# A two-layer trunk on one core: the first up projection's channels in two parts, and one more column group in the first quarter

## The chip, the cores and the metric

The kernel runs on one core of a Trainium2 chip, as one launch. The metric is the time of an execution in microseconds on the device; the smaller the better.

## The reference

The trunk has two layers on 256 tokens of 2048 channels, all in float32. The first layer mixes tokens by pooling, the second by attention; each ends with a gated feed-forward part with a convolution of width 3. A conditioning vector gives each layer six vectors of 2048 numbers, in this order: shift, scale and gate of the mixer (chunks 0, 1, 2), shift, scale and gate of the feed-forward part (chunks 3, 4, 5).

```python
cond = silu(c)
for i in range(2):
    mod = cond @ w_ada[i] + b_ada[i]              # 2048 x 12288
    sh1, sc1, g1, sh2, sc2, g2 = split(mod, 6)
    h = rmsnorm(x, norm_g[i, 0]) * (1 + sc1) + sh1
    y = pool_mixer(h) if i == 0 else moba_attention(h)
    x = x + g1 * y
    h = rmsnorm(x, norm_g[i, 1]) * (1 + sc2) + sh2
    u = causal_conv3(h @ w_up[i]) + conv_b[i]     # 2048 x 11264
    val, gate = split(u, 2)
    x = x + g2 * ((silu(gate) * val) @ w_down[i]) # 5632 x 2048
return rmsnorm(x, final_g)
```

The pool mixer handles four groups of 512 channels with one matrix each.

## The kernel before

Tokens stand transposed: channels on the partitions, 256 tokens along the row (`xT`). All weights, some 554 MB, are read once, in loads of 1 MB on SyncE's queue, into five tiles that take turns (`raw`, `RAW` = 5): load number n+5 waits until load n's tile has been read by its last reader. The program is a list of events, each a load and its use. `later` and `at` hang further work on an event. A scheduler then sets the order of instructions on each engine, each engine works in that fixed order, and semaphores hold it where data or a tile is missing.

**The conditioning stage** comes first. A chunk of the conditioning is made in slices of 512 channels: four loads (`slice_load`, tile `ws<chunk>_<slice>_<quarter>`) of four blocks of 128 rows each. A block is multiplied by its column of `cond` and added up either on VectorE (`accs`, 128x512) or, for the blocks in `PE_BLOCKS`, on TensorE (`row`, one matmul of one row of 512). `mods` matmuls turn the sums into columns and `mod_done` adds the bias. The slices run 3, 2, 1, 0 and each takes the chunks 1, 0, 2. With chunks 1 and 0 of a slice the pool group can be made (`pool_h`, `pool_sums`, `pool_less`, and 32 instructions `pp` of `pool_product` on TensorE), with chunk 2 its output is added to `xT` (`pool_out`), and `squares` collects the squares for the next norm. Then `x1` makes the norm's factor (`ms`, `st_*`, `rrow`). Slice 0 of chunks 4 and 3 follows in eight loads, and then the first step of the dense stream.

**The dense stream.** A step takes one megabyte of weights, 512 rows by 512 columns: ACT rounds it in two halves (`hi`), VectorE makes the rest (`lo`), and TensorE issues 48 matmuls on `h` (`uv` for value columns, `ug` for gate columns). `hi` and `lo` have four buffers each (`HB`), and products run two halves behind (`LAG`). The first up projection of layer 0 goes through `FIRST` = 11 column groups four times, once per quarter of its 2048 rows (K), since the conditioning of the later channels isn't there yet. The sums of the first `HOMES` = 10 groups leave PSUM after each quarter (`to_home`: ACT copies the first quarter, VectorE adds the others to `home`), the eleventh stays in PSUM. Slices 1 to 3 of chunks 3 and 4 come as pairs between these steps, eight loads a slice, all on VectorE (`accs` 128x1024). `h_blocks` makes four blocks of `h` for each quarter (`ht` on VectorE, `h` on ACT, the low part on VectorE). In the last quarter the steps alternate with those of two more groups (`MIX`), and the convolutions of finished groups run beside. After that all products are step by step, layer after layer.

Most instructions are recorded at line 50 of the profile (the helper that issues them), so rows are told apart by their tiles.

Of the kernel before, what the change touches and what calls it, by code (L numbers as in the profile page):

```python
# [17 lines left out]
P = 128  # L18
# [38 lines left out]
def trunk(ctx: ExitStack, tc: tile.TileContext, x, c, norm_g, w_ada, b_ada, pool_w, pool_scale, w_qkv, w_o,  # L57
          rel_table, w_up, conv_w, conv_b, w_down, final_g, out):
    nc = tc.nc
# [19 lines left out]
    PE_BLOCKS = ((2, 5, 8, 11, 14), (3, 7, 11, 15), (2, 4, 6, 9, 11, 13, 15), (2, 5, 7, 10, 13, 15), ())  # L79
    RAW, HB, LAG, T4, PRIO = 5, 4, 2, 6, 1000  # L80

# [160 lines left out]
    def slice_load(ch, s, q, pair):  # L242
# [10 lines left out]
        return load  # L253

    def slice_use(ch, s, q, pair):

        on_pe = PE_BLOCKS[ch if ch < 3 else 3 if s == 0 else 4]
        nk, w = (2, 2) if pair else (4, 1)

        def use(r):  # L260
            if q == 0:
                ada["n"] = ada.get("n", -1) + 1
                if ada["n"] == 0:
                    ada["acc"] = wt([P, D], "acc", 1, "accs")
                if on_pe:
                    ada["row"] = [bank(f"row{ch}_{s}_{j}") for j in range(w)]
            odd = ada["n"] % 2
# [14 lines left out]
            if nk * (q + 1) == KD:  # L282
                with tc.high_priority(offset=2 * PRIO):
                    if on_pe:
                        for j in range(w):
                            ac.activation(row[0:1, j * C:(j + 1) * C], ps[j][0:1, :], AF.Copy)
                    ps = ada["ps", ch, s] = aux(f"mods{ch}_{s}")
# [150 lines left out]
    def group_T(src, nk, c0, rhs, done, name, home=None, each=None):  # L438
# [27 lines left out]

        def products(f, k, hi, lo):
            o = part(f)
            first = k % 4 if home else k
            for kk in range(2):  # L470
# [4 lines left out]
                pe.matmul(o, lo[:, kk, w], h[:, 0:S], start=False,  # L475
                                 stop=(k + kk == nk - 1 or (home is not None and first + kk == 3)),
                                 skip_group_check=True)

        def use_of(k0):
# [73 lines left out]
    PARTS = ((0, 4), (4, 8), (8, NG))  # L553
    HOMES, FIRST, LEAD = 10, 11, 3
    REST, MIX, PRE, SPARE = 1, 2, 2, 2
    QUIET, LATE, START = 7, -0.2, 61

    def ffn(l):
        led = 0
        for pi, (ga, gb) in enumerate(PARTS):  # L560
# [46 lines left out]
            if pi == 0:  # L607
# [3 lines left out]
                if l == 0 and MIX:  # L611
# [402 lines left out]

    later = {}
    for s in range(4)[::-1]:
        e0 = len(events)
        for n, e in enumerate(e for ch in (1, 0, 2) for e in slice_events(ch, s, False)):
            event(*e)
            if n == 5:  # L1020
                event(pool_load(s), lambda r: None)
        e1 = len(events)
        at(e0 + 5, lambda s=s: slice_done(1, s, False))
        at(e0 + 9, lambda s=s: slice_done(0, s, False))
        at(e0 + 9, lambda s=s: pool_h(s))
        at(e0 + 10, lambda s=s: pool_sums(s))
        at(e0 + 10, lambda s=s: pool_less(s))
        for f in range(GB):
            at(e0 + 10 + f, lambda s=s, f=f: pool_product(s, f))
        at(e1 + 1, lambda s=s: slice_done(2, s, False))  # L1030
        at(e1 + 1, lambda s=s: pool_out(s))
        at(e1 + 2, lambda s=s: squares(s * GB, GB, s == 3))
        at(e0 + 1, {3: pool_start, 2: lambda: load_conv(0), 1: lambda: load_conv(1), 0: bias_rows}[s])

# [5 lines left out]

    at(e1 + 3, x1)
    slices = [slice_events(4, 0, False) + slice_events(3, 0, False)] + [slice_events(3, s, True) for s in range(1, 4)]
    for e in slices[0]:
        event(*e)
    at(len(events) - 3, lambda: slice_done(4, 0, False))
    i = 0
    for s in range(4):
        nxt = slices[s + 1] if s < 3 else []
        for g in range(FIRST):
            event(w_load(i), w_use(i))  # L1050
            i += 1
            if g == 0:
                at(len(events) - 1, lambda s=s: (slice_done(3, s, s > 0), h_blocks(0, 1, 4 * s, 4)))
            while nxt and (FIRST - SPARE) * (8 - len(nxt)) < 8 * (g + 1):
                event(*nxt.pop(0))
# [34 lines left out]
    FAST, MANY = 40, 14  # L1090
    PE_ON, VE_ON, AC_ON = (), (59, 60, 61), (55, 59, 60, 61)
    first_main = 200
# [40 lines left out]
```

## Time and profile before

| | us |
|---|---|
| median of 3 runs | 2071.87 (2071.46 to 2075.88) |
| the profiled execution | 2076.08 |
| its span in the profile | 2074.3 |
| TensorE busy | 2013.0 |
| VectorE busy | 1641.4 |
| ACT busy | 960.2 |

The profile shows one execution. Its span runs from the first to the last instruction; 1.78 us of that execution's time lie around it. The mean granted clock of TensorE over the span is 0.981.

### The profile page before, as it was taken

The numbers are of one execution on the slowest core, as the hardware profiler recorded it, in microseconds if no ns is written. First come the engines' busy times: TensorE is split into PE (matmuls) and PEld (weight loads), VectorE is DVE, ScalarE is ACT, GpSimd is POOL, SyncE is SP. The second block draws the span as 40 slices with busy tenths as digits, with TensorE's granted clock in tenths as the row PEclk, the third lists the DMA queues.
The fourth block names the chain that finished last, engine by engine and source line by source line (L and its number), as shares of the span: only waits on it lengthen the run. The fifth ranks groups of instructions, "written<-read, shape, count | busy, mean of one in ns | idle before, by whom it ended". The sixth has DMA issues, their size and how long they took to land. (4 is left out here: it accounts for less than half of the span.)

```text
span 2074.3 us, 38497 instructions
## 1 busy us (share of the span) xinstructions
PE 2013.0 (97%) x16292; PEld 1907.9 (92%) x16292; DVE 1641.4 (79%) x2023; ACT 960.2 (46%) x1206; POOL 12.0 (1%) x64
## 2 busy tenths in 40 slices
PE   6898999999999999999999999999999999999998
PEld 2445999999999999999989889999999999999998
DVE  6887899899889999997787887879885666556666
ACT  3112534566454345444444444446543555435454
POOL 1000000000000000000000000000000000000000
PEclk8988999999999999999999999999999999999999
DMA  9998999655997989896888788678875555556551
GB/s 355 346 363 324 345 346 326 222 191 196 336 360 279 377 320 320 305 324 213 311 288 326 265 308 313 223 250 284 280 268 187 200 195 192 197 189 200 187 202 62
DMA packets 236445, 558.78 MB, mean 269 GB/s; under 512 B 9272, under 2 KB 9592, under 8 KB 221680
## 3 DMA queue, kind: packets, MB, share of 16 engines
q1 hardware_dynamic: 234800, 553.17, 75.4%
q8 instruction: 127, 2.08, 0.4%
q0 software_dynamic: 896, 2.49, 0.3%
q10 hardware_dynamic: 576, 0.67, 0.1%
q14 instruction: 46, 0.38, 0.0%
HBM read 554.17 MB, written 2.12 MB: 268 GB/s over the span
## 5 line engine op out<-in xcount | busy, mean ns | idle before, releaser
L50 DVE TENSOR_TENSOR lo<-w,hi 128x1024 fp32r<-128x1024 f32 x656 | 790.9, 1221 | 260.0 <-ACT hi L50 259.1
L50 ACT ACTIVATE hi<-w 128x1024 fp32r<-128x1024 f32 x656 | 683.2, 1059 | 630.5 <-PE d L50 185.6
L50 PE MATMUL uv<-h,hi 128*128 128x256 f32 x2816 | 485.1, 278 | 3.8 <-ACT h L50 3.8
L50 PE MATMUL d<-act,hi 128*128 128x256 f32 x2816 | 482.0, 277 | 0.6 <-ACT hi L50 0.6
L50 PE MATMUL ug<-h,hi 128*128 128x256 f32 x2816 | 481.8, 276 | 0.0
L50 PEld LDWEIGHTS uv<-h,hi 128*128 128x128 f32 x2816 | 426.6, 189 | 4.5 <-ACT h L50 4.1
L50 PEld LDWEIGHTS d<-act,hi 128*128 128x128 f32 x2816 | 424.9, 188 | 0.9 <-ACT hi L50 0.8
L50 PEld LDWEIGHTS ug<-h,hi 128*128 128x128 f32 x2816 | 424.0, 188 | 0.0
L50 PE MATMUL d<-act,lo 128*128 128x256 f32 x1408 | 387.4, 277 | 4.0 <-DVE lo L50 4.0
L50 PE MATMUL uv<-h,lo 128*128 128x256 f32 x1408 | 387.9, 277 | 0.0
L50 PE MATMUL ug<-h,lo 128*128 128x256 f32 x1408 | 386.3, 276 | 0.0
L50 PEld LDWEIGHTS d<-act,lo 128*128 128x128 f32 x1408 | 263.9, 188 | 4.8 <-DVE lo L50 4.8
L50 PEld LDWEIGHTS uv<-h,lo 128*128 128x128 f32 x1408 | 265.1, 189 | 0.0
L50 PEld LDWEIGHTS ug<-h,lo 128*128 128x128 f32 x1408 | 263.5, 188 | 0.0
L50 DVE SCALAR_TENSOR_TENSOR acc<-wa,cond,acc 128x2048 f32<-128x2048 f32 x105 | 246.3, 2346 | 6.6 <-DMA wa<-in_w_ada_dram 6.3
L50 DVE SCALAR_TENSOR_TENSOR accs<-ws,cond,accs 128x512 f32<-128x512 f32 (+1 forms) x179 | 157.4, 882 | 17.2 <-ACT accs L50 7.9
L50 PE MATMUL k<-h,hi 128*128 128x256 f32 x512 | 93.7, 285 | 1.1 <-ACT h L50 1.1
L50 PE MATMUL row<-ws,cond 128*1 128x512 f32 x152 | 81.5, 663 | 8.3 <-DMA ws<-in_w_ada_dram 8.3
L50 PE MATMUL q<-h,hi 128*128 128x256 f32 x512 | 88.7, 278 | 0.0
L50 PE MATMUL wo<-o,hi 128*128 128x256 f32 x512 | 88.3, 277 | 0.0
L50 PEld LDWEIGHTS k<-h,hi 128*128 128x128 f32 x512 | 80.1, 191 | 2.3 <-ACT h L50 1.4
L50 PE MATMUL v<-hi,h 128*128 128x512 f32 x256 | 80.1, 394 | 0.0
(157 smaller groups left out, 1753.9 us busy)
## 6 DMA issues: line engine op xcount, KB each, us to landing
w<-in_w_up_dram SPq DMA_DIRECT2D x176, 1024.0 KB, 5.1
wa<-in_w_ada_dram SPq DMA_DIRECT2D x112, 1024.0 KB, 5.8
w<-in_w_down_dram SPq DMA_DIRECT2D x88, 1024.0 KB, 5.1
ws<-in_w_ada_dram SPq DMA_DIRECT2D x56, 1024.0 KB, 7.6
w<-in_w_qkv_dram SPq DMA_DIRECT2D x48, 1024.0 KB, 6.4
ws<-in_w_ada_dram SPq DMA_DIRECT2D x48, 512.0 KB, 6.5
w<-in_w_o_dram SPq DMA_DIRECT2D x16, 1024.0 KB, 6.8
pw<-in_pool_w_dram SPq DMA_DIRECT2D x4, 1024.0 KB, 9.0
```

Source lines behind the costliest of these rows:

```text
L50: ins = call(*args, **kwargs)
```

## The change

The last two slices of chunks 0 to 2 are taken in another order: chunks 1 and 0 of slice 1, chunks 1 and 0 of slice 0, then chunk 2 of slice 1 and of slice 0. The squares of slice 0 are no longer added on VectorE but summed by eight more `ms` matmuls.

Slice 0 of chunks 4 and 3 comes in two parts of 256 channels (`half_load`, tiles `wh<slice>_<part>_<quarter>`), each with four loads of 1 MB in two transfers with runs of 1 KB, both chunks side by side (`rowh`, `modsh`). The first part stands ahead of the first step, the second part's loads alternate with the first steps. The first quarter's ten column groups are done in ten pair steps: a step takes two groups on half of the quarter's rows (256), first all on the first half, then all on the second, so that the first five steps need the first 256 channels only. The sums go to `home` after each half. `HOMES` goes from 10 to 11, `FIRST` from 11 to 12 and the tiles `t4` from 6 to 7. The count of steps stays as it is.

```diff
-    RAW, HB, LAG, T4, PRIO = 5, 4, 2, 6, 1000
+    RAW, HB, LAG, T4, PRIO = 5, 4, 2, 7, 1000
...
+    def half_load(s, part, q):
+
+        def load():
+            r = raw_tile(f"wh{s}_{part}_{q}")
+            rows = w_ada[0, q * 4 * P:(q + 1) * 4 * P, :].rearrange("(k p) d -> p k d", p=P)
+            for j in range(2):
+                c0 = (4 - j) * D + s * C + part * C // 2
+                nc.sync.dma_start(r.rearrange("p (k j c) -> p k j c", k=4, j=2)[:, :, j, :], rows[:, :, c0:c0 + C // 2])
+            return r
+        return load
+
+    def half_events(s, part):
+        return [(half_load(s, part, q), slice_use(("half", part), s, q, False)) for q in range(4)]
+
+    def half_done(s, part):
+        ps = ada.pop(("ps", ("half", part), s))
+        for j in range(2):
+            mod_done(0, 4 - j, 4 * s + 2 * part, 2, ps[:, 2 * j:2 * j + 2])
...
-        on_pe = PE_BLOCKS[ch if ch < 3 else 3 if s == 0 else 4]
+        on_pe = PE_BLOCKS[3 if type(ch) is tuple else ch if ch < 3 else 4]
...
+        def use_two(k0, hi, lo):
+
+            box["g"] = math.inf
+            box["a"] = [bank(f"{name}_{b}") for b in range(2)]
+            for f in range(4):
+                products(f, k0, hi, lo, True)
+            to_home(k0)
+
+        twos[src.tensor.name, c0] = use_two
...
-    HOMES, FIRST, LEAD = 10, 11, 3
+    HOMES, FIRST, LEAD = 11, 12, 3
...
+                if l == 0:
+                    one = rows.pop(0)
+                    even = HOMES - HOMES % 2
+                    for k0 in (0, 2):
+                        for a, b in zip(one[0:even:2], one[1:even:2]):
+                            uses = [twos[p[0].tensor.name, p[2]] for p in (a, b)]
+                            steps.append((a[0], k0, (a[2], b[2]),
+                                          lambda half, hi, lo, k0=k0, uses=uses: uses[half](k0, hi, lo)))
+                    steps.extend(one[even:])
...
+            if type(c0) is tuple:
+                for h, c in enumerate(c0):
+                    nc.sync.dma_start(r[:, h * 2 * C:(h + 1) * 2 * C].rearrange("p (k c) -> p k c", k=2),
+                                      src[k0 * P:(k0 + 2) * P, c:c + C].rearrange("(k p) c -> p k c", p=P))
+                return r
...
+    order = [(ch, s) for s in (3, 2) for ch in (1, 0, 2)] + [(ch, s) for s in (1, 0) for ch in (1, 0)] + [(2, 1), (2, 0)]
+    for ch, s in order:
+        if ch == 1:
+            at(len(events) + 1, {3: pool_start, 2: lambda: load_conv(0), 1: lambda: load_conv(1), 0: bias_rows}[s])
+        for q, e in enumerate(slice_events(ch, s, False)):
+            event(*e)
+            if (ch, q) == (0, 1):
+                event(pool_load(s), lambda r: None)
+        last[ch, s] = len(events) - 1
...
+            at(last[0, s] + 2 + f, lambda s=s, f=f: pool_product(s, f))
+    for s in range(4)[::-1]:
+        e = last[2, s] + (2 if s else 1)
+        at(e, lambda s=s: slice_done(2, s, False))
+        at(e, lambda s=s: pool_out(s))
+        at(e + 1 if s else e, lambda s=s: squares(s * GB, GB, s == 3, s == 0))
...
-    slices = [slice_events(4, 0, False) + slice_events(3, 0, False)] + [slice_events(3, s, True) for s in range(1, 4)]
-    for e in slices[0]:
+    at(last[2, 0] + 2, x1)
+    for e in half_events(0, 0):
         event(*e)
-    at(len(events) - 3, lambda: slice_done(4, 0, False))
+    second = half_events(0, 1)
+    slices = [slice_events(3, s, True) for s in range(1, 4)]
     i = 0
+    ones_at = len(events)
+    for g in range(HOMES // 2):
+        event(w_load(i), w_use(i))
+        i += 1
+        if g == 0:
+            at(len(events) - 1, lambda: (half_done(0, 0), h_blocks(0, 1, 0, 2)))
+        if second:
+            event(*second.pop(0))
     for s in range(4):
-        nxt = slices[s + 1] if s < 3 else []
-        for g in range(FIRST):
+        nxt = slices[s] if s < 3 else []
+        n = FIRST if s else FIRST - HOMES // 2
+        for g in range(n):
             event(w_load(i), w_use(i))
             i += 1
-            if g == 0:
-                at(len(events) - 1, lambda s=s: (slice_done(3, s, s > 0), h_blocks(0, 1, 4 * s, 4)))
-            while nxt and (FIRST - SPARE) * (8 - len(nxt)) < 8 * (g + 1):
+            if g == 0 and s:
+                at(len(events) - 1, lambda s=s: (slice_done(3, s, True), h_blocks(0, 1, 4 * s, 4)))
+            elif g == 0:
+                at(len(events) - 1, lambda: (half_done(0, 1), h_blocks(0, 1, 2, 2)))
+            while nxt and (n - SPARE) * (8 - len(nxt)) < 8 * (g + 1):
```

On TensorE, before the change, this is the place behind the pool products of the last group (`pp0`): what stands there is the first part of chunk 4, slice 0 (`row4_0_0`).

```order
L50 MATMUL pp0_1_924<-pool_room_231,pw0_824 128x256 x4
L50 MATMUL pp0_0_923<-pool_room_231,pw0_824 128x256 x5
L50 MATMUL pp0_1_924<-pool_room_231,pw0_824 128x256
L50 MATMUL row4_0_0_961<-ws4_0_0_891,cond_94 1x512
L50 MATMUL row4_0_0_961<-ws4_0_1_914,cond_94 1x512 x2
L50 MATMUL row4_0_0_961<-ws4_0_2_929,cond_94 1x512
L50 MATMUL row4_0_0_961<-ws4_0_3_939,cond_94 1x512 x2
L50 MATMUL mods4_0_1001<-ones_74,accs_206 128x1 x4
```

After the change the products of the last pool group stand ahead of `row` matmuls of chunk 2, slice 0.

```order
L50 MATMUL pp0_1_877<-pool_room_231,pw0_771 128x256 x3
L50 MATMUL pp0_0_876<-pool_room_231,pw0_771 128x256 x5
L50 MATMUL pp0_1_877<-pool_room_231,pw0_771 128x256 x2
L50 MATMUL mods2_0_958<-ones_74,accs_206 128x1 x3
L50 MATMUL ms_990<-mean_c_84,sqa12_419 128x1
L50 MATMUL mods2_0_958<-ones_74,accs_206 128x1
L50 MATMUL ms_990<-mean_c_84,sqa12_419 128x1
L50 MATMUL row2_0_0_915<-ws2_0_0_844,cond_94 1x512
L50 MATMUL row2_0_0_915<-ws2_0_1_867,cond_94 1x512 x2
L50 MATMUL row2_0_0_915<-ws2_0_2_882,cond_94 1x512 x2
```

Behind the pool block stood the rows of chunk 4; now the rows of chunk 2 stand there, a chunk that is loaded earlier. The next place is TensorE just ahead of the first product of the up projection (`uv0_0_0`), here before the change.

```order
L50 MATMUL mods4_0_1001<-ones_74,accs_206 128x1 x4
L50 MATMUL ms_1010<-mean_c_84,sqa12_419 128x1 x2
L50 MATMUL row3_0_0_1032<-ws3_0_2_982,cond_94 1x512
L50 MATMUL row3_0_0_1032<-ws3_0_3_994,cond_94 1x512 x2
L50 MATMUL rrow_1024<-ident_69,st_r2_1022 128x128 x2
L50 MATMUL mods3_0_1060<-ones_74,accs_206 128x1 x8
L50 MATMUL uv0_0_0_1107<-h0_1_1029,hi0_0_1071 128x256
```

The same place after the change, where `rowh0` and `rowh1` are the rows of the two half slices and `modsh0` turns the sums of the first.

```order
L50 MATMUL ms_990<-mean_c_84,sq0_981 128x1 x8
L50 MATMUL rrow_1012<-ident_69,st_r2_1010 128x128
L50 MATMUL modsh0_0_1033<-ones_74,accs_206 128x1 x4
L50 MATMUL rrow_1012<-ident_69,st_r2_1010 128x128
L50 MATMUL rowh1_0_0_1067<-wh0_1_0_983,cond_94 1x512
L50 MATMUL modsh0_0_1033<-ones_74,accs_206 128x1 x4
L50 MATMUL rowh1_0_0_1067<-wh0_1_1_1025,cond_94 1x512 x2
L50 MATMUL uv0_0_0_1079<-h0_1_1017,hi0_0_1045 128x256
```

Eight `ms` matmuls, the half slices' `row` and `mods` now stand there; the rows of `wh0_1_2`, `wh0_1_3` and the matmuls `modsh1` follow behind the first `uv`. On VectorE the place ahead of the first `ht01_0` reads so before:

```order
L50 SCALAR_TENSOR_TENSOR accs_206<-ws3_0_3_994,cond_94,accs_206 128x512 x2
L50 TENSOR_TENSOR lo0_0_1072<-w0_1030,hi0_0_1071 128x1024
L50 TENSOR_TENSOR lo0_1_1076<-w0_1030,hi0_1_1075 128x1024
L50 TENSOR_TENSOR mod_113<-mods3_0_1060,bT_189 128x4
L50 SCALAR_TENSOR_TENSOR ht01_0_1080<-xT_100,gsc_114,rrow_1027 128x256
```

and so after:

```order
L50 SCALAR_TENSOR_TENSOR st_r2_1010<-st_q_1007,st_r_1005 128x2
L50 TENSOR_TENSOR lo0_0_1046<-w0_967,hi0_0_1045 128x1024
L50 TENSOR_TENSOR lo0_1_1050<-w0_967,hi0_1_1049 128x1024
L50 TENSOR_TENSOR mod_113<-modsh0_0_1033,bT_189 128x2
L50 TENSOR_TENSOR lo1_0_1076<-w1_1018,hi1_0_1075 128x1024
L50 SCALAR_TENSOR_TENSOR gsc_114<-mod_113,vecs_185 128x2
L50 TENSOR_TENSOR mod_113<-modsh0_0_1033,bT_189 128x2
L50 TENSOR_TENSOR lo1_1_1106<-w1_1018,hi1_1_1105 128x1024
L50 SCALAR_TENSOR_TENSOR ht01_0_1056<-xT_100,gsc_114,rrow_1015 128x256
```

Two `lo` stood ahead of the first `ht`, now four do. The third place is VectorE where the blocks of `h` for the second quarter begin (`ht01_4`); before:

```order
L50 SCALAR_TENSOR_TENSOR accs_206<-ws3_1_7_1431,cond_94,accs_206 128x1024 x2
L50 TENSOR_TENSOR lo8_0_1582<-w8_1436,hi8_0_1581 128x1024
L50 TENSOR_TENSOR lo8_1_1591<-w8_1436,hi8_1_1590 128x1024
L50 TENSOR_TENSOR mod_113<-mods3_1_1569,bT_189 128x4 x2
L50 SCALAR_TENSOR_TENSOR gsc_114<-mod_113,vecs_185 128x4
L50 SCALAR_TENSOR_TENSOR ht01_4_1834<-xT_100,gsc_114,rrow_1027 128x256
```

After:

```order
L50 TENSOR_TENSOR lo13_0_1986<-w13_1767,hi13_0_1985 128x1024
L50 TENSOR_TENSOR lo13_1_1992<-w13_1767,hi13_1_1991 128x1024
L50 SCALAR_TENSOR_TENSOR accs_206<-ws3_2_1_1833,cond_94,accs_206 128x1024
L50 TENSOR_TENSOR mod_113<-mods3_1_1758,bT_189 128x4 x2
L50 SCALAR_TENSOR_TENSOR accs_206<-ws3_2_1_1833,cond_94,accs_206 128x1024
L50 SCALAR_TENSOR_TENSOR gsc_114<-mod_113,vecs_185 128x4
L50 SCALAR_TENSOR_TENSOR accs_206<-ws3_2_2_1978,cond_94,accs_206 128x1024
L50 SCALAR_TENSOR_TENSOR ht01_4_1962<-xT_100,gsc_114,rrow_1015 128x256
```

The second quarter's `mod` and `ht01_4` stood behind the halves of step 8 and now stand behind those of step 13; the accumulations of the slice after (`ws3_2`) lie between.

## Rows read from the trace of the kernel before

**Rows 1.** The page, part 1: busy time of two engines, share, instructions.

```profile
PE 2013.0 (97%) x16292; PEld 1907.9 (92%) x16292; DVE 1641.4 (79%) x2023; ACT 960.2 (46%) x1206; POOL 12.0 (1%) x64
```

**Rows 2.** Windows: length, busy PE, PEld, DVE, ACT, POOL; PEclk, DMA share, GB/s.

```profile
207.00:264.00 57.00, 57.00 (x504) 57.00 (x503) 47.66 (x48) 34.38 (x46) 0.00 (x0) 1.00 0.94 343
220.00:240.00 20.00, 20.00 (x179) 20.00 (x178) 16.37 (x15) 12.08 (x16) 0.00 (x0) 1.00 1.04 401
460.00:500.00 40.00, 40.00 (x355) 40.00 (x354) 40.00 (x63) 26.68 (x36) 0.00 (x0) 1.00 0.62 209
875.00:900.00 25.00, 23.13 (x190) 22.93 (x189) 23.25 (x30) 10.58 (x11) 0.00 (x0) 0.93 0.81 284
925.00:950.00 25.00, 22.56 (x168) 21.71 (x167) 18.88 (x37) 11.61 (x18) 0.79 (x1) 0.86 0.50 172
```

**Rows 3.** GB/s in 40 equal slices of 0.75 us, 165 to 195 us.

```profile
GB/s 404 415 410 404 410 410 410 407 407 415 396 180 46 14 0 0 0 0 0 0 0 0 0 106 273 382 390 344 281 333 380 380 355 374 390 385 396 407 404 412
```

**Rows 4.** TensorE's timeline: start, length, instructions, idle before and what ended it.

```profile
162.30 0.65 PE L50 MATMUL xh<-ident,x 128*128 128x128 f32 x4
...
170.89 9.48 PE L50 MATMUL pp<-pool_room,pw 128*128 128x256 f32 x32
180.30 5.31 PE L50 MATMUL row<-ws,cond 128*1 128x512 f32 x12
...
190.16 0.61 PE L50 MATMUL ms<-mean_c,sqa 128*128 128x1 f32 x4
...
196.37 0.71 PE L50 MATMUL rrow<-ident,st_r 128*128 128x128 f32 x4
196.91 1.93 PE L50 MATMUL mods<-ones,accs 128*128 128x1 f32 x16
201.58 1.10 PE L50 MATMUL uv<-h,hi 128*128 128x256 f32 x3 [2.73 <-ACT h L50]
```

**Rows 5.** SyncE's queue from 181 us, and one load's issue to landing (us, last column).

```profile
181.39 2.90 SPq L251 DMA_DIRECT2D ws<-in_w_ada_dram  x3
...
ws<-in_w_ada_dram SPq DMA_DIRECT2D x1, 1024.0 KB, 5.0
```

**Rows 6.** VectorE's timeline, 167 to 202 us.

```profile
167.78 1.22 DVE L50 TENSOR_TENSOR pool_room<-pool_room 128x1024 f32<-128x1024 f32 x1
...
181.42 0.87 DVE L50 SCALAR_TENSOR_TENSOR xT<-pp,gate,xT 128x256 f32<-128x256 f32 x2
...
198.10 2.36 DVE L50 TENSOR_TENSOR lo<-w,hi 128x1024 fp32r<-128x1024 f32 x2 [3.32 <-ACT hi L50]
...
200.45 0.87 DVE L50 SCALAR_TENSOR_TENSOR ht<-xT,gsc,rrow 128x256 f32<-128x256 f32 x2
```

**Rows 7.** ACT's timeline, 182 to 200 us.

```profile
182.33 1.06 ACT L50 ACTIVATE sq<-xT 128x1024 f32<-128x1024 f32 x1 [14.55 <-DVE xT L50]
...
196.53 0.59 ACT L50 ACTIVATE accs<-row 1x512 f32<-1x512 f32 x1 [5.46 <-PE row L50]
197.03 1.99 ACT L50 ACTIVATE hi<-w 128x1024 fp32r<-128x1024 f32 x2
198.92 0.36 ACT L50 ACTIVATE rrow<-rrow 128x256 f32<-128x256 f32 x1
```

**Rows 8.** VectorE's timeline at the second quarter's blocks and at additions to home.

```profile
248.19 0.23 DVE L50 TENSOR_TENSOR mod<-mods,bT 128x4 f32<-128x4 f32 x2 [1.93 <-PE mods L50]
248.45 0.16 DVE L50 SCALAR_TENSOR_TENSOR gsc<-mod,vecs 128x4 f32<-128x4 f32 x1
248.65 0.88 DVE L50 SCALAR_TENSOR_TENSOR ht<-xT,gsc,rrow 128x256 f32<-128x256 f32 x2
...
268.03 1.28 DVE L50 SCALAR_TENSOR_TENSOR accs<-ws,cond,accs 128x1024 f32<-128x1024 f32 x1
269.23 0.68 DVE L50 TENSOR_TENSOR home<-home,uv 128x512 f32<-128x512 f32 x1
269.83 1.28 DVE L50 SCALAR_TENSOR_TENSOR accs<-ws,cond,accs 128x1024 f32<-128x1024 f32 x1
```

More of the change, by code (lines that the diff above doesn't have):

```diff
@@ L253, in slice_load @@
         return load
+    def half_load(s, part, q):
[13 more added lines that the diff above has]
+            mod_done(0, 4 - j, 4 * s + 2 * part, 2, ps[:, 2 * j:2 * j + 2])
     def slice_use(ch, s, q, pair):
-        on_pe = PE_BLOCKS[ch if ch < 3 else 3 if s == 0 else 4]
+        on_pe = PE_BLOCKS[3 if type(ch) is tuple else ch if ch < 3 else 4]
+        name = f"h{ch[1]}" if type(ch) is tuple else ch
         nk, w = (2, 2) if pair else (4, 1)
@@ L265, in use @@
                 if on_pe:
-                    ada["row"] = [bank(f"row{ch}_{s}_{j}") for j in range(w)]
+                    ada["row"] = [bank(f"row{name}_{s}_{j}") for j in range(w)]
             odd = ada["n"] % 2
@@ L286, in use @@
                             ac.activation(row[0:1, j * C:(j + 1) * C], ps[j][0:1, :], AF.Copy)
-                    ps = ada["ps", ch, s] = aux(f"mods{ch}_{s}")
+                    ps = ada["ps", ch, s] = aux(f"mods{name}_{s}")
                     for j in range(4 * w):
@@ L412, in trunk @@
     groups = [0]
+    twos = {}
     def after(i, f):
@@ L465, in to_home, with products @@
             defer(2, adds)
-        def products(f, k, hi, lo):
+        def products(f, k, hi, lo, alone=False):
             o = part(f)
-            first = k % 4 if home else k
+            first = 0 if alone else k % 4 if home else k
             for kk in range(2):
@@ L475, in products @@
                 pe.matmul(o, lo[:, kk, w], h[:, 0:S], start=False,
-                                 stop=(k + kk == nk - 1 or (home is not None and first + kk == 3)),
+                                 stop=(k + kk == nk - 1 or (home is not None and first + kk == (1 if alone else 3))),
                                  skip_group_check=True)
+        def use_two(k0, hi, lo):
[5 more added lines that the diff above has]
+        twos[src.tensor.name, c0] = use_two
         def use_of(k0):
@@ L1015, in trunk @@
     later = {}
-    for s in range(4)[::-1]:
[L1017 to L1027, printed above, removed]
-        for f in range(GB):
[L1029 to L1033, printed above, removed]
+    last = {}
+    order = [(ch, s) for s in (3, 2) for ch in (1, 0, 2)] + [(ch, s) for s in (1, 0) for ch in (1, 0)] + [(2, 1), (2, 0)]
[7 more added lines that the diff above has]
+        last[ch, s] = len(events) - 1
+    for s in range(4)[::-1]:
+        at(last[1, s] + 2, lambda s=s: slice_done(1, s, False))
+        at(last[0, s] + 1, lambda s=s: slice_done(0, s, False))
+        at(last[0, s] + 1, lambda s=s: pool_h(s))
+        at(last[0, s] + 2, lambda s=s: pool_sums(s))
+        at(last[0, s] + 2, lambda s=s: pool_less(s))
+        for f in range(GB):
+            at(last[0, s] + 2 + f, lambda s=s, f=f: pool_product(s, f))
[4 more added lines that the diff above has]
+        at(e + 1 if s else e, lambda s=s: squares(s * GB, GB, s == 3, s == 0))
     def x1():
@@ L1039, in x1 @@
         new_h("h0_1")
-    at(e1 + 3, x1)
-    slices = [slice_events(4, 0, False) + slice_events(3, 0, False)] + [slice_events(3, s, True) for s in range(1, 4)]
-    for e in slices[0]:
+    at(last[2, 0] + 2, x1)
+    for e in half_events(0, 0):
         event(*e)
-    at(len(events) - 3, lambda: slice_done(4, 0, False))
+    second = half_events(0, 1)
+    slices = [slice_events(3, s, True) for s in range(1, 4)]
     i = 0
+    ones_at = len(events)
[6 more added lines that the diff above has]
+            event(*second.pop(0))
     for s in range(4):
-        nxt = slices[s + 1] if s < 3 else []
-        for g in range(FIRST):
+        nxt = slices[s] if s < 3 else []
+        n = FIRST if s else FIRST - HOMES // 2
+        for g in range(n):
             event(w_load(i), w_use(i))
             i += 1
-            if g == 0:
-                at(len(events) - 1, lambda s=s: (slice_done(3, s, s > 0), h_blocks(0, 1, 4 * s, 4)))
-            while nxt and (FIRST - SPARE) * (8 - len(nxt)) < 8 * (g + 1):
+            if g == 0 and s:
[3 more added lines that the diff above has]
+            while nxt and (n - SPARE) * (8 - len(nxt)) < 8 * (g + 1):
                 event(*nxt.pop(0))
@@ L1090, in trunk @@
     FAST, MANY = 40, 14
-    PE_ON, VE_ON, AC_ON = (), (59, 60, 61), (55, 59, 60, 61)
+    PE_ON, VE_ON, AC_ON = (), (ones_at - 1, ones_at, ones_at + 1), (ones_at - 5, ones_at - 1, ones_at, ones_at + 1)
     first_main = 200
```

## The prediction

> **What bounds the kernel now.** I read the busy table first: TensorE is busy for 97% of the span, VectorE for 79% [rows 1]. By stretches: from 207 us to 264 us TensorE runs without a gap at full clock, 504 matmuls in 57.00 us, so a step of 48 takes 5.43 us [rows 2]. The end is therefore set by three things: when the first product of the up projection starts (201.58 us [rows 4]), what else TensorE must do behind it, and gaps in the dense stream. Before that start the loads should be the bound, but the line of GB/s shows a hole: the transfers run at some 410, then stand still from about 174 us to 182 us [rows 3]. The order says why: the next load takes the tile of `ws4_0_0`, whose last reader is a `row` matmul queued behind the 32 `pp` matmuls of the pool mixer, which hold TensorE from 170.89 us for 9.48 us; that `row` starts at 180.30 us [rows 4], SP issues the load at 181.39 us and it takes 5.0 us to land [rows 5]. VectorE has 15 to 20% of slack in the first stretches and none at 460 to 500 us [rows 2].
>
> **The change, part by part.**
>
> *The start (A).* Four megabytes leave the stretch ahead of the first product, 2.6 us each at the 401 GB/s of 220 to 240 us [rows 2], so one would expect it 10.5 us earlier. The order speaks against that. The hole stays, only four loads earlier in the stream: `wh0_0_1` takes the tile of `ws2_0_0`, whose `row` matmul now stands behind the same pool block, and as many loads follow the hole up to `w0` as before. Its time: the last transposes `xh` at 162.30 us move up by the eight `mods` matmuls no longer ahead of them, 1.93 us [rows 4], to 160.4. From them to the end of the last `pool_room` subtraction it took 6.7 us (169.0 − 162.3 [rows 4, 6]): 167.1. Pool products 9.5: 176.6. Four `mods` and two `ms` matmuls in between, about 1.4: 178.0. The first `row`, 0.9 (12 instructions, two per matmul, in 5.31 us [rows 4]): 178.9, issued 179.1, landed 184.1 [rows 5].
> From there a chain that was spread out now lies end to end. Seven `row` matmuls are done at about 184.2; those of `wh0_0_0` and `wh0_0_1` end at 186.9 and the last four `mods2_0` at 187.9. VectorE's mod, gate and one accumulation, 1.0: 188.9. Pool output in two pairs at 0.87 [rows 6]: 190.6. ACT's square 1.06 [rows 7]: 191.7. Sixteen `ms` instructions at a quarter of 0.61 for four, 2.4 but pipelined with the wait, 1.7: 193.4. The root and its reciprocal, about 1.2: 194.6. `rrow` and its `mods` 0.71 + 1.0 [rows 4] less overlap: 196.2. ACT's two copies, 0.36 and 0.59: 197.2; then four `hi`, 1.0 each [rows 7]: 201.2. VectorE makes four `lo` at 1.18 [rows 6] ahead of the first `ht`, where before two stood there; the last ends 2 us behind ACT's last `hi`: 203.2. From `ht` to the first product 1.13 (200.45 to 201.58 [rows 4, 6]): 204.3. So **+2.7 us**. Bounds: the loads alone (184.1 + 6 × 2.6 + 1.8 for `hi`, `lo`) give 201.5, so 0; the 18.2 us that before took from the pool output's end (182.29) to `ht` (200.45 [rows 6]) in place of my 12.6 give +8.3.
>
> *Runs of 1 KB in the half loads.* No row has them. Between nothing (all bytes at 401 GB/s) and twice the time (a run of 1 KB as long as one of 2 KB, 5.2 us a half load) lie, after the slack of about 2 us, up to +8 at the start. I take nothing: in the stretch with 401 GB/s three of eight megabytes came in transfers of 512 KB, and the queue was full [rows 2]. The Trainium skill (DMA: Bandwidth & Descriptors, section Bandwidth) says to batch DMAs to 1 MiB or more for 75% of peak; by its figure of 341 GB/s at 1 MB, three half loads ahead of the start would, as an estimate, be 0.5 us slower each, +1.5 in all. The row decides, since several transfers overlap on the queue.
>
> *Work moved behind the start (B).* Three `row` matmuls (0.89 each) and eight `modsh1` (1.93 [rows 4]) now run after the first product, between products: **+4.6 us**, certain, since TensorE is full there.
>
> *The boundary between the first and second quarter of K (C).* The second quarter needs `ht01_4` and so the sums of channels 512 to 1023. Before, their `mod` stands at `lo8`, three steps ahead of the boundary, at 248 us, and costs nothing. After the change the eight loads of that slice come later and the order puts `mod` and `ht01_4` behind `lo13_0` and `lo13_1` and three accumulations of the next slice. With four buffers of `lo`, `lo13` waits for the last product of step 11, which is the last of the first quarter. So when TensorE has done it, VectorE still has to do: `lo` 1.18, three accumulations 1.20 each, mod and gsc 0.3, `ht` 0.44 [rows 6, 8], then 0.7 to the product: 6.2 us, less the 1 to 1.9 of `mods` matmuls that TensorE has in it, so at least 4.5. The steps on half of K bring VectorE 20 `home` additions that the first quarter didn't have (there ACT only copied). In that stretch its work (24 `lo`, 20 `home` at 0.60, 19 accumulations at 1.20, 9 of half that size and small ones [rows 6, 8]) is about 72 us against TensorE's 12 × 5.43 + 7 = 72, so it may be late by more, up to 10. Were VectorE not full there, these additions would lie beside the products and cost nothing. I take **+7.5 us** (bounds 0, if TensorE's lag lets VectorE catch up, and 10).
>
> *The clock after that wait (D).* Where TensorE idles 1.87 of 25 us, the granted clock is 0.93 of its upper level (2.4 GHz), so a part of the stretch ran at the lower one (1.2 GHz); where 2.44, it is 0.86 [rows 2]. 0.07 and 0.14 of 25 us are 1.75 to 3.5 us of work lost. **+2** (0 to 3.5).
>
> *The last quarter (E).* With one home more, 20 steps carry the convolutions that 23 carried, and VectorE is already full there, 40.00 of 40 us [rows 2]. **+1.5** (0 to 5, a `lo` a step late). The pair steps read the same megabyte and issue the same 48 matmuls as a whole step (two groups on two blocks of K instead of one on four), so they are costed at nothing beyond their `home` additions; if a pair step cost more, all ten lie in the open on TensorE. Steps, bytes and products are else as many as before; the eight extra `ms` matmuls lie in the chain of A.
>
> *Sum.* 2.7 + 4.6 + 7.5 + 2 + 1.5 = +18.3, on the profiled execution's 2076.08: 2094.4. That execution lies 4.2 above the median of the runs shown, so I give 2071.87 + 18.3 = 2090.2.
>
> **The rivals.** *The boundary is hidden:* VectorE gains on TensorE in the first quarter, because TensorE starts late and has `row` work in between. Then C and D are nothing: +8.8, 2080.7. Against it, `lo13` can't run ahead whatever VectorE gains.
> *The start gains, the boundary costs:* −10.5 in place of +2.7 gives +5.1, 2077.0.
> *The other side, faster:* the loads don't stop, the first product comes 10.5 us earlier, and the boundary is covered: −10.5 + 4.6 = −5.9, 2066.0. For that the first `row2_0_0` would have to run by about 168 us instead of 178; break-even with the moved work at a start near 197 us. Against it stands the queue order alone, which is fixed. By the Trainium skill (the same page, section Specifications) HBM gives a core 358 GB/s; as an estimate the four megabytes would then be worth 11.7 us and this case 2064.8. The row's 401 GB/s says that this core isn't held to that.
> *Half a gain:* a start some 5 us earlier and a covered boundary cancel: 2072.
> *More late halves:* VectorE doesn't recover behind the boundary or E reaches its bound: over 2101.
>
> **How the numbers follow.** Forecast 0.60, boundary hidden 0.16, start gained with the boundary 0.08, faster 0.08, half a gain 0.04, over 2101 0.04. 0.2% is 4.1 us, about what a measurement can tell from no change. Faster: 0.08 and a little of half a gain, 0.09. Same: the rest of that and the parts of the second and third case that end below +4.1, 0.11. Slower 0.80. The range takes the forecast with its bounds, the hidden boundary and the start gained: 2075 (B alone, with small change) to 2101 (C and D at their upper bounds, A half way to its own); outside it are 0.16.
>
> **What would show it.** A: the GB/s line falls to nothing from about 164 to 179 us, the load that ends it is a `wh`, and the first `uv` stands near 204 us; a start before 198 makes this step wrong. B: `row` and `mods` matmuls within the first 25 us behind the first `uv`. C: TensorE idle for 5 to 10 us near 275 to 285 us, ended by ACT's `h`; no such idle makes it wrong. D: a stretch with a granted clock under 0.95 there. E: TensorE waits for `lo` between 470 and 540 us. If half loads cost more than I take, the DMA share is high while the GB/s are under 380.

## The result and the profile after

The changed kernel takes 2098.80 us (median of 4 runs, 2093.66 to 2099.93) against 2073.88 (4 runs of before, 2071.46 to 2076.06): a ratio of 1.0106, 95% interval 1.0093 to 1.0120. It is slower, as forecast, and stands inside the range; the size was forecast at 18.3 us and is 24.9 by the medians, 23.3 by the spans of the profiled executions (2097.6 against 2074.3).

The busy times of the changed kernel, as in [rows 1]:

```profile
PE 2022.9 (96%) x16308; PEld 1914.1 (91%) x16308; DVE 1655.0 (79%) x2048; ACT 963.3 (46%) x1208; POOL 11.9 (1%) x64
```

TensorE is busy for 9.9 us more and idle for 13.4 us more. Where, a count tells: in the groups of TensorE's matmuls I counted the `uv` and `ug` rows up to a time, and took the time at which the n-th has come, for each kernel. The table gives that time less the one of before, in us.

```
n-th product               1      48      96     144     480     570     624    2600
before, us            201.58  209.37  214.82  220.25  260.17  270.36  276.49  504.11
changed kernel         +7.36   +6.17  +10.33  +11.95  +10.10  +10.12  +22.64  +23.04
pool_behind_rows       -3.68   -3.22   +0.94   +0.96   -0.89   -0.87   +9.85  +12.16
three_pairs            +6.86   +7.63  +11.71  +11.71   +9.87  +11.69  +11.69  +11.84
two_pairs_pool         -0.83   -1.11   +0.88   +6.81   +6.91   +6.91   +6.91   +6.94
before_pool_split      +0.51   +2.57   +2.57   +2.58   +2.61   +2.63   +2.61   +4.64
old_order              -2.24   -1.13   +3.10   +3.12   +1.82   +2.50  +14.94  +14.98
old_order_three_pairs  -4.12   -1.85   +0.32   +0.34   -1.49   +0.33   +0.33   +0.32
no_second_home_add     +7.33   +6.22  +10.36  +12.00  +12.10  +12.10  +12.08  +12.07
homes_alone            +2.82   +2.70   +2.69   +2.69   +2.68   +2.68   +2.68   +2.67
order_alone            +8.39   +8.57   +8.55   +8.57   +8.57   +8.57   +8.57   +8.55
ht_ahead               +5.72   +4.58   +7.78  +10.72   +8.89   +8.89  +22.22  +23.24
pool_pairs_ht          -5.28   -5.80   -3.65   -1.47   -3.31   -1.49   +0.20   +0.41
order_pairs_ht         -0.41   +0.05   +2.16   +4.27   +4.62   +6.44   +8.15   +8.33
```

The changed kernel loses in three places and nowhere else: 7.4 us before the first product, 5.8 between the 48th and the 144th, 12.5 at the 576th, which is the end of the first quarter. Of the last, 1.95 are `mods` matmuls that before had earlier (the step back at 480). The first place, in GB/s of 155 to 200 us (slices of 1.125 us):

```profile
GB/s 402 413 406 410 408 406 409 379 385 259 15 1 0 0 0 0 0 0 0 0 0 0 0 2 226 379 363 293 358 359 378 379 396 410 390 382 399 408 401 388
```

and on SyncE's queue (start, length):

```profile
160.53 24.81 SPq L262 DMA_DIRECT2D wh<-in_w_ada_dram  x8
180.96 4.38 SPq L262 DMA_DIRECT2D wh<-in_w_ada_dram  x6
```

The hole of [rows 3] has grown: transfers stand from about 167 to 181 us. The first row holds eight issues as one; the second, of a narrower window, shows that six of them come only from 180.96 us on, behind the `row` matmul that frees their tile. TensorE there, answering to [rows 4], and below it at the end of the first quarter:

```profile
162.26 0.60 PE L50 MATMUL xh<-ident,x 128*128 128x128 f32 x4
162.70 1.93 PE L50 MATMUL mods<-ones,accs 128*128 128x1 f32 x16
169.10 9.60 PE L50 MATMUL pp<-pool_room,pw 128*128 128x256 f32 x32 [4.48 <-DVE pool_room L50]
...
179.86 6.17 PE L50 MATMUL row<-ws,cond 128*1 128x512 f32 x14
...
198.80 1.71 PE L50 MATMUL modsh<-ones,accs 128*128 128x1 f32 x8
200.37 0.78 PE L50 MATMUL rrow<-ident,st_r 128*128 128x128 f32 x2
201.07 1.86 PE L50 MATMUL rowh<-wh,cond 128*1 128x512 f32 x2
202.87 1.86 PE L50 MATMUL modsh<-ones,accs 1*128 1x1 f32 x8
204.66 3.57 PE L50 MATMUL rowh<-wh,cond 128*1 128x512 f32 x4
208.92 0.50 PE L50 MATMUL uv<-h,hi 128*128 128x256 f32 x2 [0.69 <-ACT h L50]
...
282.53 1.95 PE L50 MATMUL mods<-ones,accs 128*128 128x1 f32 x16 [1.11 <-DVE accs L50]
290.19 0.79 PE L50 MATMUL uv<-h,hi 128*128 128x256 f32 x2 [5.71 <-ACT h L50]
```

The row that lets the loads go on starts at 179.86, behind the pool block, and the first product at 208.92. VectorE ahead of the start, answering to [rows 6], and at the end of the first quarter, answering to [rows 8]:

```profile
189.71 1.54 DVE L50 SCALAR_TENSOR_TENSOR accs<-wh,cond,accs 128x512 f32<-128x512 f32 x2 [1.70 <-DMA wh<-in_w_ada_dram]
191.17 0.15 DVE L50 TENSOR_TENSOR mod<-mods,bT 128x4 f32<-128x4 f32 x1
...
277.71 2.37 DVE L50 TENSOR_TENSOR lo<-w,hi 128x1024 fp32r<-128x1024 f32 x2
279.99 2.49 DVE L50 SCALAR_TENSOR_TENSOR accs<-ws,cond,accs 128x1024 f32<-128x1024 f32 x2
282.38 2.38 DVE L50 TENSOR_TENSOR lo<-w,hi 128x1024 fp32r<-128x1024 f32 x2
284.64 1.30 DVE L50 SCALAR_TENSOR_TENSOR accs<-ws,cond,accs 128x1024 f32<-128x1024 f32 x1
285.84 0.25 DVE L50 TENSOR_TENSOR mod<-mods,bT 128x4 f32<-128x4 f32 x2
285.98 1.30 DVE L50 SCALAR_TENSOR_TENSOR accs<-ws,cond,accs 128x1024 f32<-128x1024 f32 x1
287.18 0.17 DVE L50 SCALAR_TENSOR_TENSOR gsc<-mod,vecs 128x4 f32<-128x4 f32 x1
287.91 1.28 DVE L50 SCALAR_TENSOR_TENSOR accs<-ws,cond,accs 128x1024 f32<-128x1024 f32 x1 [0.56 <-DMA ws<-in_w_ada_dram]
289.11 0.88 DVE L50 SCALAR_TENSOR_TENSOR ht<-xT,gsc,rrow 128x256 f32<-128x256 f32 x2
```

TensorE's products end at 281.4 us; VectorE works on without a gap up to the late load and reaches `ht` at 289.11. The windows of the changed kernel around these places (columns as in [rows 2]):

```profile
208.92:212.00 3.08, 3.08 (x27) 3.08 (x28) 2.88 (x5) 0.97 (x2) 0.00 (x0) 1.00 1.04 368
...
224.00:232.00 8.00, 8.00 (x57) 7.99 (x57) 4.95 (x10) 6.01 (x9) 0.00 (x0) 0.79 0.85 302
224.00:228.00 4.00, 4.00 (x24) 3.99 (x24) 2.76 (x7) 2.46 (x4) 0.00 (x0) 0.66 0.89 340
...
281.50:290.19 8.69, 1.95 (x17) 1.86 (x17) 8.13 (x12) 1.47 (x3) 0.00 (x0) 0.80 1.02 380
290.19:297.50 7.31, 7.08 (x33) 6.79 (x34) 5.95 (x9) 1.26 (x3) 0.00 (x0) 0.54 1.05 403
...
460.00:500.00 40.00, 40.00 (x355) 40.00 (x355) 38.54 (x61) 26.34 (x35) 0.00 (x0) 1.00 0.57 187
```

At the boundary TensorE is idle for 6.7 us of 8.69, and the 7.08 us behind it run at 0.54 of the clock: 3.3 us more.

### The profile page after: what moved, and what is told of

It is laid out like the page before. It is cut to its first block, busy times and chain, and to the rows that moved or that the text cites. A ratio compares the mean times of both kernels' runs of the same rounds, so it can differ in the third digit from the quotient of the medians.

```text
span 2097.6 us, 38602 instructions
## 1 busy us (share of the span) xinstructions
PE 2022.9 (96%) x16308; PEld 1914.1 (91%) x16308; DVE 1655.0 (79%) x2048; ACT 963.3 (46%) x1208; POOL 11.9 (1%) x64
## 5 line engine op out<-in xcount | busy, mean ns | idle before, releaser
L50 DVE SCALAR_TENSOR_TENSOR accs<-ws,cond,accs 128x512 f32<-128x512 f32 (+1 forms) x161 | 144.2, 899 | 24.4 <-DMA ws<-in_w_ada_dram 12.7
L50 PEld LDWEIGHTS wo<-o,hi 128*128 128x128 f32 x512 | 77.2, 188 | 0.1
```

The lines of the kernel that those rows point to most:

```text
L50: ins = call(*args, **kwargs)
```

## The experiments

The theory: the new order lets the pool block stop the loads early (the start), and VectorE, loaded with 20 `home` additions, is late at the boundary. Rivals: the half loads are slow; the boundary waits for loads; the eleventh home costs.

**The pool block behind the rows** (the changed kernel with)

```diff
-            at(last[0, s] + 2 + f, lambda s=s, f=f: pool_product(s, f))
+            at(last[0, s] + (2 if s else 5) + f, lambda s=s, f=f: pool_product(s, f))
```

> The changed kernel with the last pool group's products hung three events later, so that the row matmuls of chunk 2, slice 0 stand ahead of them on TensorE. Theory (the hole in the loads sets the start): the first row2_0_0 runs before 168 us, the GB/s line has no stretch at nothing longer than 5 us between 160 and 185 us, the first uv stands at 196 to 201 us in place of 208.9, the boundary stays; total 2086 to 2092. Rival (the half loads with runs of 1 KB, or the chain of the norm, set the start): first uv at 206 to 210 us, total 2096 to 2101.

Measured: 2090.50 us, 1.0085 (1.0063 to 1.0106) of before, 8.3 under the changed kernel's median. TensorE's rows:

```profile
165.42 5.31 PE L50 MATMUL row<-ws,cond 128*1 128x512 f32 x12
170.66 5.02 PE L50 MATMUL pp<-pool_room,pw 128*128 128x256 f32 x22
...
197.90 0.80 PE L50 MATMUL uv<-h,hi 128*128 128x256 f32 x2 [1.48 <-ACT h L50]
```

The `row` matmuls are through before the block starts, and the first product comes 11.0 us earlier with the same half loads. The late start is the pool block's doing. In the table the boundary still costs 10.7 (-0.87 to +9.85).

**Three pairs in place of five** (the changed kernel with the following; the loads are shared out to match)

```diff
-                    even = HOMES - HOMES % 2
+                    even = 6
...
-    for g in range(HOMES // 2):
+    for g in range(3):
...
-        if second:
+        while second and (g == 2 or len(second) > 3 - g * 4 // 3):
...
-        n = FIRST if s else FIRST - HOMES // 2
+        n = FIRST if s else FIRST - 3
```

> The changed kernel with six column groups in pair steps (three and three steps) in place of ten, the other groups of the first quarter as whole steps, so 12 home additions in place of 20; the last two half loads come together behind the third step. Theory (VectorE's additions push mod and ht behind the boundary): TensorE's idle time at the end of the first quarter falls from 6.8 us to under 1.5 and the clock doesn't fall there; total 8 to 12 us under the changed kernel, 2087 to 2091. Rival (the boundary waits for the slice's loads, which come as late as before): idle 5 us or more, total 2095 to 2101. The first uv stays at 208 to 210 us in both.

Measured: 2084.78 us, 1.0054 (1.0035 to 1.0072), 14.0 under the changed kernel's median and 2.2 under the range expected; its profile is 11.2 us earlier at the 2600th product. VectorE and the window at the boundary:

```profile
273.73 0.23 DVE L50 TENSOR_TENSOR mod<-mods,bT 128x4 f32<-128x4 f32 x2 [0.71 <-PE mods L50]
...
274.19 0.88 DVE L50 SCALAR_TENSOR_TENSOR ht<-xT,gsc,rrow 128x256 f32<-128x256 f32 x2
```

```profile
280.00:290.00 10.00, 10.00 (x91) 10.00 (x90) 10.00 (x12) 4.29 (x5) 0.00 (x0) 1.00 0.98 361
```

`ht` comes at 274.19 in place of 289.11; TensorE has no gap, and the clock stays full. Here the slice's loads also spread over more steps, so VectorE's additions are not yet told from the loads.

**No addition after the second half.** `to_home` is called for `k0 == 0` alone; 20 additions are left out of the output, the loads stay where they were.

```diff
-            to_home(k0)
+            if k0 == 0:
+                to_home(k0)
```

> The changed kernel without the 20 additions to home after the second half of the first quarter (these sums are left out of the output). Theory (VectorE is the bound at the boundary): the first uv at 208 to 210 us as in the changed kernel, the idle time at the end of the first quarter under 1.5 us, total 2085 to 2090. Rival (loads of the slice come too late): idle 5 us or more, total 2094 to 2101.

Measured: 2089.08 us (2 runs), 1.0073 (1.0049 to 1.0097), 9.7 under the changed kernel. First product at 208.91, no wait of TensorE between 260 and 330 us. With the loads in their places the boundary is free: the additions are the cause, and the rival falls. VectorE there:

```profile
268.80 0.23 DVE L50 TENSOR_TENSOR mod<-mods,bT 128x4 f32<-128x4 f32 x2 [1.40 <-PE mods L50]
...
269.26 0.88 DVE L50 SCALAR_TENSOR_TENSOR ht<-xT,gsc,rrow 128x256 f32<-128x256 f32 x2
```

How the additions act, this run doesn't separate, because without them the scheduler also gave `ht` another place. Counted on VectorE from 185 us, the second quarter's first `ht` stands behind 22 `lo` and 15 accumulations (128x1024) here, behind 24 and 15 with three pairs, and behind 28 and 19 in the changed kernel. There the 28th `lo` is `lo13_1`, and ACT can make its `hi` only when the last products of the quarter free the buffer:

```profile
281.34 1.06 ACT L50 ACTIVATE hi<-w 128x1024 fp32r<-128x1024 f32 x1 [0.80 <-PE ug L50]
```

This `hi` is done at 282.40 us, and VectorE comes to the `lo` some 1.1 us later (the second of the pair from 282.38). So by this trace VectorE's backlog itself costs about 1.1 us, and the place in its order, behind `lo13_1` and three accumulations, the rest. No run has the additions with `ht` in its earlier place.

**The order of before** (the changed kernel with the loop over slices of the kernel before, and the work hung on it)

```diff
-    order = [(ch, s) for s in (3, 2) for ch in (1, 0, 2)] + [(ch, s) for s in (1, 0) for ch in (1, 0)] + [(2, 1), (2, 0)]
...
-    at(last[2, 0] + 2, x1)
+    for s in range(4)[::-1]:
+        e0 = len(events)
+        for n, e in enumerate(e for ch in (1, 0, 2) for e in slice_events(ch, s, False)):
...
+    at(e1 + 3, x1)
```

> The changed kernel with the slices' order of before (and squares added on VectorE as before); halves, pair steps and eleven homes stay. Theory (the new order moved the hole in the loads ahead of the loads that the start needs): first uv at 193 to 198 us, the row and mods matmuls behind it still cost 4 to 6 us, the boundary 10 to 12 us; total 2080 to 2088. Rival (the half loads make the start late): first uv at 204 us or later, total 2094 or more.

Measured: 2088.19 us, 1.0067 (1.0048 to 1.0086). First product at 199.31, 9.6 earlier than in the changed kernel though 1.3 outside what was expected; the total lies 0.2 above the range expected, and the boundary (12.4) 0.4 above its own.

**The new order alone** (the kernel before with)

```diff
-        for n, e in enumerate(e for ch in (1, 0, 2) for e in slice_events(ch, s, False)):
...
+    order = [(ch, s) for s in (3, 2) for ch in (1, 0, 2)] + [(ch, s) for s in (1, 0) for ch in (1, 0)] + [(2, 1), (2, 0)]
...
+        at(e + 1 if s else e, lambda s=s: squares(s * GB, GB, s == 3, s == 0))
```

> The kernel before with the new order of the last two slices and the squares apart, nothing else (whole loads of slice 0, ten homes). Theory (the order puts the hole four loads earlier, and eight whole loads and the first step's now follow it): first uv at 206 to 212 us, nothing lost behind it, total 2077 to 2084. Rival (the norm's chain sets the start, the order is harmless): first uv at 200 to 203 us, total 2071 to 2076.

Measured: 2085.47 us, 1.0048 (1.0031 to 1.0064), 1.5 above the range expected; first product at 209.95, +8.4, and the table's line stays flat behind it. So the order alone makes a start that late, without a half load. The last link differs: with eight whole loads behind the hole, ACT rounds the first step at 205.40 us (`hi`), in the changed kernel at 201.94.

**The homes alone** (the kernel before with)

```diff
-    RAW, HB, LAG, T4, PRIO = 5, 4, 2, 6, 1000
+    RAW, HB, LAG, T4, PRIO = 5, 4, 2, 7, 1000
...
-    HOMES, FIRST, LEAD = 10, 11, 3
+    HOMES, FIRST, LEAD = 11, 12, 3
```

> The kernel before with eleven homes, twelve groups in the first quarters and seven t4 tiles, nothing else. Theory: the start as before (201 to 202 us), VectorE a little denser in the last quarter, total 2071 to 2077. Rival (the additional home is what costs): 2078 to 2085.

Measured: 2074.68 us, 1.0007 (0.9995 to 1.0019): no change that can be told. Its profiled execution starts 2.8 us late, with the pool block at 173.39 in place of 170.89 and the same rows ahead of it; the line is flat behind. By the line the eleventh home costs nothing.

**`ht` ahead of the second step's `lo`** (the changed kernel with)

```diff
-    PE_ON, VE_ON, AC_ON = (), (ones_at - 1, ones_at, ones_at + 1), (ones_at - 5, ones_at - 1, ones_at, ones_at + 1)
+    PE_ON, VE_ON, AC_ON = (), (ones_at - 1, ones_at, ones_at + 1, ones_at + 2), (ones_at - 5, ones_at - 1, ones_at, ones_at + 1)
```

> The changed kernel with one number more in the list of events that VectorE keeps in program order, so that the first ht stands behind two lo, as before, and not behind four. Theory (the two lo are a part of the late start): first uv 2 to 3 us earlier, 206 to 207 us, total 2094 to 2098. Rival (ht waits for the row or the mods matmuls anyway): first uv at 208 to 210 us, total as the changed kernel.

Measured: 2099.34 us, 1.0114 (1.0091 to 1.0136), 1.3 above the range expected. The first product comes at 207.28, 1.6 earlier (0.9 of it because the pool block ended earlier in this execution). The gain is given back: TensorE waits 8.31 us for ACT's `h` at the boundary, where `uv` starts at 290.41, as late as in the changed kernel.

**Undoing several costs.** The following runs combine the edits above. Two pairs (the diff of three pairs with 4 and 2 in place of 6 and 3) with the pool block behind the rows:

```diff
-                    even = HOMES - HOMES % 2
+                    even = 4
...
-            at(last[0, s] + 2 + f, lambda s=s, f=f: pool_product(s, f))
+            at(last[0, s] + (2 if s else 5) + f, lambda s=s, f=f: pool_product(s, f))
```

> Both edits: the pool products behind the rows, and four column groups in pair steps (8 home additions). Theory: both gains add up, first uv 196 to 201 us and no boundary wait; total 2074 to 2083, so still not under the kernel before, since the row and mods matmuls behind the start and the clock remain. Rival (each gain is given back, because the second half's conditioning is late for the third step): a new wait of 5 us or more near 215 to 225 us, total 2084 to 2092.

Measured: 2080.66 us, 1.0028 (1.0014 to 1.0042). Both gains are there (200.74, no boundary wait), and the rival's wait too, though smaller: 2.4 us idle between 200 and 222 us, and the window around that wait at a low clock:

```profile
216.00:224.00 8.00, 5.62 (x24) 5.33 (x25) 7.93 (x10) 2.27 (x4) 0.00 (x0) 0.62 1.05 391
```

The order of before with three pairs:

> The order of before and six column groups in pair steps. Theory: first uv at 193 to 198 us and no boundary wait, 4 to 6 us of row and mods matmuls behind the start; total 2069 to 2076, about as the kernel before. Rival (a wait for the second half's conditioning takes the gain): a wait of 4 us or more between 205 and 225 us, total 2077 to 2082.

Measured: 2079.15 us (2071.99 to 2085.55), 1.0024 (1.0008 to 1.0039): in the rival's range, but its profiled execution (span 2076.0) has no wait between 205 and 225 us and is within 0.4 us of before in the table. Its other executions lie between 5.8 us under the profiled one and 7.7 above it, and no profile shows where they differ; that stays open. Pool block, three pairs and `ht` together:

> The three edits that undo a cost, together: pool products behind the rows, three pairs, ht ahead of the second step's lo. Theory: first uv at 194 to 197 us, 4 to 6 us of row and mods matmuls behind it, no boundary wait; total 2068 to 2075, level with the kernel before. Rival (the second half's conditioning comes too late for the fourth step): a wait of 3 us or more at 205 to 225 us, total 2076 to 2081.

Measured: 2077.51 us, 1.0010 (0.9998 to 1.0021), not told apart from before. The time lies in the rival's range, without the rival's wait: in the profile the start is at 196.29, then 4.3 are lost to row and mods matmuls and 1.4 to a wait for `h` between 270 and 300 us, and the end is 0.4 behind before. The order of before, three pairs and `ht`:

> The order of before, three pairs, ht ahead of the second step's lo. Theory: first uv at 194 to 197 us, total 2068 to 2075. Rival as for the run with the pool products: a wait at 205 to 225 us, total 2076 to 2081.

Measured: 2081.31 us, 1.0019 (1.0005 to 1.0032); its profiled execution ended the pool block only at 183.3 us, the run with the order of before at 179.0, so its start (201.15) lies outside the 194 to 197 expected. No version beats the kernel before.

**The pool block of before, split** (the kernel before with)

```diff
-            at(e0 + 10 + f, lambda s=s, f=f: pool_product(s, f))
+            at(e0 + (10 if s else 15) + f, lambda s=s, f=f: pool_product(s, f))
...
-        at(e1 + 1, lambda s=s: pool_out(s))
+        at(e1 + (1 if s else 6), lambda s=s: pool_out(s))
...
-    at(e1 + 3, x1)
+    at(e1 + 7, x1)
```

> The kernel before, with the last pool group's products hung five events later and its output and squares (by eight more ms matmuls) behind them: half of the pool block then stands behind the rows of chunk 4. Theory (the hole sets the start there too): the hole from 174 to 182 us is split or shorter, first uv at 195 to 199 us in place of 201.6, total 2066 to 2071. Rival (the chain from the pool's output over the norm sets the start, and it is now later): first uv at 202 to 206 us, total 2072 to 2078.

Measured: 2082.31 us, 1.0041 (1.0028 to 1.0054). The GB/s of 155 to 200 us:

```profile
GB/s 386 410 406 408 406 417 386 404 408 408 408 410 410 408 408 410 408 410 291 167 351 408 406 410 406 411 408 408 381 282 386 357 320 355 320 401 324 62 15 0
```

The hole is gone, and the first product still comes at 202.07, after 4.88 us of waiting for ACT's `h`. The edit has made the other chain to that product later: the pool's last addition ends at 185.52 us in place of 182.29, and `rrow` waits for the norm's factor (`st_r`).

```profile
184.64 0.88 DVE L50 SCALAR_TENSOR_TENSOR xT<-pp,gate,xT 128x256 f32<-128x256 f32 x2 [2.16 <-PE pp L50]
...
195.70 0.16 DVE L50 SCALAR_TENSOR_TENSOR st_r<-st_q,st_r 128x2 f32<-128x2 f32 x1
196.00 1.19 PE L50 MATMUL rrow<-ident,st_r 128*128 128x128 f32 x4 [1.29 <-DVE st_r L50]
```

So here the chain over pool output and norm sets the start, as the rival has it (202 to 206). That the hole is covered in the kernel before doesn't follow. There VectorE and TensorE wait for loads behind the hole, and `rrow` (196.37 in [rows 4]) stands on TensorE behind this `row`, while the factor is ready at 193.33:

```profile
190.47 0.75 DVE L50 SCALAR_TENSOR_TENSOR accs<-ws,cond,accs 128x512 f32<-128x512 f32 x1 [2.47 <-DMA ws<-in_w_ada_dram]
193.10 3.34 PE L50 MATMUL row<-ws,cond 128*1 128x512 f32 x4 [1.38 <-DMA ws<-in_w_ada_dram]
193.17 0.16 DVE L50 SCALAR_TENSOR_TENSOR st_r<-st_q,st_r 128x2 f32<-128x2 f32 x1
```

The two chains end there within 0.3 us, and what the hole alone costs no run shows: this one traded it for a later norm. Its total lies 4.3 us above the rival's range; the table has 2.6 at the 48th product and 2.0 more between the 624th and the 2600th, and why isn't shown.

## Why the prediction was right, and where its sizes were off

**What bounds the kernel** held for the dense stream. For the start of before it is half of the answer: loads behind the hole are waited for, and the chain over the norm ends at nearly the same time, so taking the hole away gains only if that chain isn't made later.

**A, the start (+2.7 forecast, +7.36 measured, bound 8.3).** The mechanism, the pool block ahead of the `row` that frees the tile, is shown by the pool experiment from one side and by the order alone from the other. The size was off by 4.7, step by step: the transposes didn't move up by the eight `mods` (162.26, not 160.4), since other matmuls fill that place, so the pool block and everything behind it is 1.9 late; an accumulation that waits 1.70 for a `wh` load (189.71) stands ahead of chunk 2's `mod` on VectorE, 1.3; and the second half of `rrow` stands behind eight `modsh` matmuls, so ACT's copy starts at 201.18, another 1.5. That two more `lo` stand ahead of `ht` is true but cost little in the end (0.7 us in `ht_ahead`).

**Runs of 1 KB at nothing** was a little low: 354 to 386 GB/s were measured (last section), between the row's 401 and the figure of 341.

**B, the moved matmuls (+4.6).** The mechanism and its size are shown: from the start of each group to the next product, `rowh` holds TensorE for 2.76 us and `modsh` for 1.79, together 4.55. That the line from the first product to the 144th also loses 4.6 (7.36 to 11.95) is luck in part, since two things that the prediction has not lie in it. The changed kernel loses 1.7 us to a low clock (0.79 over 224 to 232 us), and the kernel before lost 2.4, because its first products ran at half the clock, where those of the changed kernel ran at full:

```profile
201.58:204.00 2.42, 2.42 (x11) 2.40 (x12) 2.35 (x5) 2.42 (x4) 0.00 (x0) 0.50 1.04 400
204.00:207.00 3.00, 3.00 (x18) 3.00 (x18) 3.00 (x5) 1.66 (x3) 0.00 (x0) 0.62 1.05 399
```

The 0.7 or 0.8 that is left of the 4.6 is not traced.

**C and D, the boundary (7.5 + 2 forecast, 12.5 measured with 1.95 of moved `mods`, so 10.6).** Idle time 6.7, clock 3.3, the rest small: C was 0.8 too high, D 1.3 too low. That the additions cause the wait is shown by leaving them out alone. C gives two reasons: the place behind `lo13_1`, and VectorE late on its own account. The trace has the first, with 1.1 us of the second; no run tells them apart. That C and D miss in opposite directions made their sum better than its parts.

**E (+1.5)** isn't there: the line rises by 0.4 from the 624th to the 2600th product, and homes alone change nothing. VectorE had 38.54 of 40 us to do from 460 to 500 us, and TensorE waited for nothing between 470 and 540.

Sum by the table: 7.4 + 4.6 - 1.85 + 12.5 + 0.4 = 23.0, the span's 23.3.

**The rivals** in which the boundary was hidden or the start gained did not come. The one on the other side named its condition rightly: with chunk 2's rows done by 170.7 us the start does move by 11 us, but to 197.90, only 3.7 ahead of before, since then the chain over the norm sets the start: `rrow` waits for `st_r` until 188.55 there, and `hi`, four `lo` and `ht` follow. Its price of 10.5 was too high by 6.8.

## What to carry to other kernels

Before giving a queue less to move, find the engine on which the release of its tiles stands: a `row` matmul behind a block of 9.6 us stops every load behind it, whatever the loads weigh. Splitting a reduction to start earlier adds a pass over its sums, and the engine that does these additions should have that time at the next boundary; if it hasn't, look at where the next block's work then stands in that engine's order, for an earlier start is given back there. And before taking a hole out of the transfers, follow every chain to the product that waits: here the hole of the kernel before was traded for a later norm, and the start stayed.

## What the runs showed of the hardware

Loads with runs of 1 KB moved 386 GB/s with the queue full (the run with the order of before, 161.5 to 166.5 us, 1403 of 1662 packets under 2 KB), those of before 406 in the same window: 5% less, 0.13 us on a megabyte. Over a quarter of the bytes in that stretch came in longer runs. With half loads alone (the run with the pool block behind the rows, 165 to 171 us, 2124 of 2125 packets under 2 KB) it was 354. Loads of before fell to 360 in one stretch too (186 to 192 us), so the length of the run isn't all that counts there. By the Trainium skill (DMA: Bandwidth & Descriptors, section Specifications) 512 B are enough for the full rate; here runs of 1 KB stayed 5 to 13% under the 406.

The granted clock fell to 0.66 between 224 and 228 us in the changed kernel while TensorE was busy for all 4.00 us: a part of it ran at 1.2 GHz. It had done `rowh` and `modsh` matmuls between its products just before, with no idle time. That these are the cause isn't shown: with three pairs the same matmuls ran between products from 214 to 224 us, and the clock stayed full from 216 to 232. And two executions with the same order of rows there (the kernel before, and it with the additional home) reach the pool block at 170.89 or at 173.39 us, which moves all behind it: a share of a run's spread lies ahead of the first product.
